# Token sums taken from rows, the next head's work at other places, and a direct attention projection, in a float32 encoder layer on one core

## The chip, the core and the metric

The program runs on one core of one Trainium2 chip. The time of a run is the device time of that core in microseconds (us). The kernel before took 1615.31 us, the median of three runs (1612.32 to 1615.61). The engines are named as the profile names them: PE (TensorE, matmul) with PEld (its weight loads), DVE (VectorE), ACT (ScalarE), POOL (GpSimd) and SP (SyncE, which issues nearly all transfers here).

## The reference

One encoder layer on x of 1024 tokens by 1024 features, all in float32. Two branches are computed from one projection, gated, added, and projected back.

```python
h = rms_norm(x, g_pre)
u_a, v_a, z_a, q_b, k_b, v_b, z_b, gate_a, gate_b = split(h @ w_in)    # 1024 -> 12288
y_a = spatial_gating(gelu(u_a), gelu(v_a), ln_g, ln_b, w_s, b_s) * silu(z_a)   # 2048 wide
y_b = mixture_of_dilations(q_b, k_b, v_b) * silu(z_b)    # 8 heads of 128, dilations 1, 4, 16
g_a, g_b = sigmoid(gate_a + b_gate[:1024]), sigmoid(gate_b + b_gate[1024:])
m = g_a * (y_a @ w_pa) + g_b * (y_b @ w_pb)
out = x + rms_norm(m @ w_o, g_post)
```

Each token attends, in each of three patterns, to 64 positions on both sides at a stride of 1, 4 or 16; the three results are combined by their softmax denominators.

## The kernel before

A float32 factor is kept as two parts, hi and lo: ACT copies the value to a rounded type (hi, L159, L106 for weights), and DVE or POOL subtracts it from the value (lo, L160, L108). A product is three matmuls: hi by hi, hi by lo, lo by hi. Nearly all of them multiply a 128x128 block by 128x512 into a PSUM bank of 128x512; there are eight banks.

The token matrix h is stored transposed, feature blocks on the partitions, in quarters hT[j][b]: j is the half of the features, b the half of the tokens. Most projections are not done directly, but by the seven products of Strassen's scheme on the 2x2 quarters, named p1, p6, p2, p7, p5, p4, p3 in that order; they need sums of token quarters (t1 to t4) and sums of weight quarters (s1 to s4, rows of the name ws_...).

The program has these stages, and pools of SBUF memory are opened and closed with them.

- Start (L202 to L330). norm_tile(c) takes one of eight chunks of 128 tokens, normalises it (ACT squares, DVE L230), transposes it on PE (L235) and splits it into hT. spatial_weights(q) prepares the spatial weights. Then v_b, which is needed in token rows, is computed directly by rows_product: chunk groups (0,1), (2,3), (4..7) with the first 512 columns, then (0..3) and (4..7) with the second. v_out splits the result into vh and vl (L160) and stores them; that frees the bank. Norms are emitted between the k steps of the first groups, and the four calls of sum_tile (L245) between those of the last two groups. sum_tile(k) adds hi and lo of a feature block on POOL (L251), forms t3, t2, t4, t1 on DVE (L257) and splits them.
- Projections (to 1033 us), seven products per block of 128 columns; gates(0) is the first. The change leaves this stage alone.
- Heads (to 1408 us). For each of eight heads weigh(h) runs nine stages: PE transposes the softmax weights (tiles st), they are split into pth and ptl (ptla for the chunked patterns), and multiplied with the values. Beside them run the next head's scores, a number of pairs of PSUM halves per stage (PAIRS), its exchange of maxima and sums between partitions, its normalise (which ends in scaling all its weights, L697 on DVE for eight of the tiles), and a number of steps of the other branch's product y_a @ w_pa (matmuls L844 to L846, bank pa, called steps).
- Tail. y_b times silu(z_b) is formed on POOL (L910) from o_d and z_d in DRAM, w_pb is read in quarters of 1 MB, and y_b @ w_pb runs as seven products (L1031 to L1033, pbp). gated() multiplies by the gate (thb), adds the other branch (mb, L987) and splits. Then the output product m @ w_o with wo's parts from DRAM (L1081 to L1083), the last norm and the residual, two chunks of tokens at a time.

The order on each engine comes from the scheduler of the language: it takes instructions of the program by their place in it, and may move one ahead where its inputs are ready in its model. Within an engine, instructions run in the order so fixed; an instruction that waits holds back all behind it, and so does a transfer in SP's queue. Tiles of a tag share a fixed number of buffers (bufs): a new one waits until the old content is no longer read.

Of the kernel before, what the change touches and what calls it, by code (L numbers as in the profile page):

```python
# [13 lines left out]
ALU = mybir.AluOpType  # L14
# [22 lines left out]
def tile_hybrid_encoder(  # L37
# [164 lines left out]
    with tc.tile_pool(name="start", bufs=1) as sp:  # L202
        xts, stored = [], []

        def load_tile(c):
            xt = sp.tile([P, D], F32, tag="xt", bufs=2, name=f"xt{c}")
            nc.sync.dma_start(xt, x_t[c])
            xts.append(xt)

        load_tile(0)  # L210
# [8 lines left out]
        def norm_tile(c, ahead=2):  # L219
            b, i = divmod(c, 4)  # L220
            for d in range(len(xts), min(c + ahead, 8)):
                load_tile(d)
            xt = xts[c]
            ss = sp.tile([P, 2], F32, tag="ss", bufs=2, name=f"ss{c}")
            xn = sp.tile([P, D], F32, tag="xn", bufs=2, name=f"xn{c}")
            nc.scalar.activation(xn, xt, AF.Square, accum_out=ss[:, 0:1])
            power(ss[:, 1:2], ss[:, 0:1], 1.0 / D)
            for j in range(2):
                gs = slice(512 * j, 512 * (j + 1))
                nc.vector.scalar_tensor_tensor(xn[:, gs], xt[:, gs], ss[:, 1:2], gpre[:, gs], op0=ALU.mult,  # L230
                                               op1=ALU.mult)
                pt = bank("pv", f"xT{c}{j}")
                for k in range(4):
                    kk = 4 * j + k
                    nc.tensor.transpose(pt[:, k * P:(k + 1) * P], xn[:, kk * P:(kk + 1) * P], ident)  # L235
                split(*[t[:, :, i * P:(i + 1) * P] for t in hT[j][b]], pt.rearrange("p (k n) -> p k n", k=4))

        def v_out(c, cb, ps):
            vh = sp.tile([P, 512], F32R, tag="vh", bufs=2, name=f"vh{cb}{c}")
# [5 lines left out]
        def sum_tile(k):  # L245

            xs = {}
            for j in range(2):
                for b in range(2):
                    xs[j, b] = sp.tile([P, 512], F32, tag=f"x{j}{b}", bufs=1, name=f"x{j}{b}_{k}")  # L250
                    nc.gpsimd.tensor_tensor(xs[j, b], f32(hT[j][b][0][:, k, :]), f32(hT[j][b][1][:, k, :]), ALU.add)  # L251
            t2 = sp.tile([P, 512], F32, tag="ssum", bufs=1, name=f"t2f{k}")
            for n, s, first, second, op in (("t3", xs[1, 1], xs[1, 1], xs[0, 1], ALU.subtract),
                                            ("t2", t2, xs[1, 1], xs[0, 0], ALU.add),
                                            ("t4", xs[1, 0], xs[1, 0], t2, ALU.subtract),
                                            ("t1", xs[0, 1], xs[0, 1], xs[0, 0], ALU.subtract)):
                nc.vector.tensor_tensor(s, first, second, op)  # L257
                if n in R:
                    split(R[n][0][:, k, :], R[n][1][:, k, :], s)
                else:  # L260
                    hl = [sp.tile([P, 512], F32R, tag=f"ss{q}", bufs=1, name=f"{n}{q}{k}") for q in "hl"]
                    split(*hl, s)
                    for t, d in zip(hl, t4_d):
                        nc.sync.dma_start(d[:, k, :], f32(t))
# [35 lines left out]
        for k in range(0, KT, 2):  # L300
            if k == 2:
                norm_tile(1, 1)
            wv += row_pair(w_in, OFF_VB, k, "vb0", (nc.gpsimd, nc.vector) if k < 4 else (nc.gpsimd, nc.gpsimd))
            if k == 0:
                load_tile(1)
            spatial_weights(k // 2)
        for cb, cs, tags in ((0, (0, 1), "mm mm"), (0, (2, 3), "sc sc"), (0, (4, 5, 6, 7), "sc tp mm mm"),
                             (1, (0, 1, 2, 3), "sc sc sc tp"), (1, (4, 5, 6, 7), "mm mm sc sc")):
            ahead = {}
            if cb == 0 and cs[0] < 4:  # L310
                ahead = {2: lambda: norm_tile(2), 5: lambda: norm_tile(3)} if cs[0] == 0 else \
                    {2 * i: (lambda c=4 + i: norm_tile(c)) for i in range(4)}
# [8 lines left out]
            if (cb, cs[0]) == (0, 4):  # L321
# [814 lines left out]
```

## Time and profile before

| What | us |
|---|---|
| median of three runs | 1615.31 |
| profiled execution | 1610.12 |
| its span, first to last instruction | 1608.3 |
| PE busy | 1508.8 |
| start, to the end of v_b | 0 to 147 |
| projections | 147 to 1033 |
| heads | 1033 to 1408.7 |
| attention projection, seven products | 1408.7 to 1499.3 |
| output product and end | 1499.3 to 1608.3 |

The profile is that of one execution. A row of the view in time order gives the start, the duration, the engine and line, the operation, "out<-in" by the program's names, the shape, and in brackets how long the engine was idle before it and what it waited for. A row of the grouped view has the busy time and the mean duration in ns of one, then the idle time before the group. A row of the transfers has the number, KB of each, and the median us from issue to landing. Matmuls overlap, so the distance of two starts counts and not the duration in the row. Lines are those of the kernel before.

### The profile page before, as it was taken

The numbers are of one execution on the slowest core, as the hardware profiler recorded it, in microseconds if no ns is written. First come the engines' busy times: TensorE is split into PE (matmuls) and PEld (weight loads), VectorE is DVE, ScalarE is ACT, GpSimd is POOL, SyncE is SP. The second block draws the span as 40 slices with busy tenths as digits, with TensorE's granted clock in tenths as the row PEclk, the third lists the DMA queues.
The fourth block names the chain that finished last, engine by engine and source line by source line (L and its number), as shares of the span: only waits on it lengthen the run. The fifth ranks groups of instructions, "written<-read, shape, count | busy, mean of one in ns | idle before, by whom it ended". The sixth has DMA issues, their size and how long they took to land.

```text
span 1608.3 us, 22594 instructions
## 1 busy us (share of the span) xinstructions
PE 1508.8 (94%) x7751; PEld 1264.2 (79%) x7751; DVE 934.6 (58%) x1698; ACT 716.0 (45%) x1391; POOL 818.5 (51%) x723
## 2 busy tenths in 40 slices
PE   8959999999999999999999999989998899789798
PEld 4747999988888888788788888767877777677586
DVE  5852544476675765757565655566666554596412
ACT  5422533343433434443354544677776665144111
POOL 3542644465555555565555555364344433687432
PEclk8979999999999999999999999999999999999899
DMA  8335433334534443536243343676666665924631
GB/s 263 136 125 191 150 106 105 111 125 133 162 125 144 135 147 116 180 102 193 99 159 130 121 148 110 217 227 196 194 198 179 207 188 168 334 97 144 235 105 66
DMA packets 238467, 252.14 MB, mean 157 GB/s; under 512 B 14056, under 2 KB 174856, under 8 KB 238096
## 3 DMA queue, kind: packets, MB, share of 16 engines
q1 hardware_dynamic: 238128, 250.14, 48.8%
q8 instruction: 61, 1.00, 0.3%
q10 hardware_dynamic: 224, 0.56, 0.1%
q14 instruction: 54, 0.44, 0.1%
HBM read 174.10 MB, written 76.55 MB: 156 GB/s over the span
## 4 chain that ended last, share of the span: by engine, by line
PE 63%; DVE 13%; DMA 6%; ACT 6%; issue 6%; POOL 5%; SPq 1%; DVEq 0%; POOLq 0%; ACTq 0%
PE sg L515 2%; PE pa L845 1%; PE pa L844 1%; PE pa L846 1%; DMA wr_pa<-in_w_proj_a_dram 1%; DMA vn<-v_d 1%; DVE vn L504 1%; PE vb L154 1%; PE vb L156 1%; PE vb L155 1%; PE sc L650 1%; ACT st L657 1%; DVE y L919 1%; ACT qrh L159 1%; PE pr L731 1%
## 5 line engine op out<-in xcount | busy, mean ns | idle before, releaser
L108 POOL TENSOR_TENSOR wl_pa<-wr_pa,wh_pa 128x512 fp32r<-128x512 f32 x56 | 73.4, 1318 | 86.7 <-ACT wh_pa L106 69.4
L504 DVE TENSOR_SCALAR vn<-vn,mean,rstd 128x128 f32<-128x128 f32 x128 | 55.3, 486 | 34.9 <-DMA vn<-v_d 34.5
L657 ACT ACTIVATE st<-st,own 128x256 f32<-128x256 f32 (+1 forms) x128 | 63.0, 493 | 24.0 <-DVE own L653 23.4
L106 ACT ACTIVATE wh_pa<-wr_pa 128x512 fp32r<-128x512 f32 x64 | 38.7, 624 | 46.1 <-DMA wr_pa<-in_w_proj_a_dram 37.2
L671 POOL COPY oth<-own 32x4 f32<-32x4 f32 x128 | 25.1, 196 | 54.1 <-ACT st L657 49.8
L653 DVE CUSTOM_DVE_ANT_0 st<-sc,tb 128x256 f32<-128x256 f32 x64 | 25.6, 422 | 37.8 <-PE sc L652 27.4
L160 POOL TENSOR_TENSOR vl<-vn,vh 128x512 fp32r<-128x512 f32 x32 | 41.3, 1292 | 0.8 <-ACT vh L159 0.8
L1085 ACT ACTIVATE sq<-o 128x512 f32<-128x512 f32 x16 | 9.6, 599 | 70.5 <-PE o L1083 70.5
L160 POOL TENSOR_TENSOR qcl<-q,qch 128x512 fp32r<-128x512 f32 x16 | 24.8, 1552 | 29.7 <-ACT qch L159 29.6
L1061 DVE TENSOR_TENSOR sso<-sso 128x1 f32<-128x1 f32 x8 | 1.3, 159 | 63.5 <-ACT sq L1085 63.5
L159 ACT ACTIVATE mhp<-mb 128x512 fp32r<-128x512 f32 x16 | 10.1, 632 | 54.9 <-POOL mb L987 54.9
L160 DVE TENSOR_TENSOR vl<-vb,vh 128x512 fp32r<-128x512 f32 x16 | 10.8, 688 | 38.2 <-ACT vh L159 33.9
L165 POOL TENSOR_TENSOR sso<-sso,mhalf 128x1 f32<-128x1 f32 x8 | 4.4, 552 | 54.9 <-DVE sso L164 54.9
L108 POOL TENSOR_TENSOR wl_wos<-wr_wos,wh_wos 128x512 fp32r<-128x512 f32 x16 | 20.7, 1293 | 22.8 <-ACT wh_wos L106 22.8
L154 PE MATMUL vb<-wh_vb,hT00h 128*128 128x512 f32 x32 | 14.2, 445 | 18.7 <-DVE vl L160 18.7
L1081 PE MATMUL o<-woh,mhp 128*128 128x512 f32 x64 | 26.3, 414 | 5.8 <-DMA woh<-wo_h 5.8
L987 POOL TENSOR_TENSOR mb<-thb,mb 128x512 f32<-128x512 f32 x16 | 21.4, 1337 | 19.8 <-DVE thb L986 15.5
L160 DVE TENSOR_TENSOR ptla<-pa,ptha 128x512 fp32r<-128x512 f32 (+1 forms) x32 | 19.8, 618 | 17.7 <-ACT ptha L159 17.6
L910 POOL TENSOR_TENSOR y<-y,zf 128x1024 f32<-128x1024 f32 x8 | 24.0, 3006 | 11.5 <-DMA zf<-z_d 8.7
L1082 PE MATMUL o<-wol,mhp 128*128 128x512 f32 x64 | 26.8, 422 | 3.1 <-DMA wol<-wo_l 3.1
L650 PE MATMUL sc<-krh,qch 128*128 128x256 f32 (+2 forms) x80 | 24.3, 306 | 5.7 <-DVE own L653 5.2
L653 DVE CUSTOM_DVE_ANT_0 st<-sc,ta 128x256 f32<-128x256 f32 x48 | 20.0, 420 | 15.2 <-PE sc L652 7.3
(2695 smaller groups left out, 6073.0 us busy)
## 6 DMA issues: line engine op xcount, KB each, us to landing
wr_pa<-in_w_proj_a_dram SPq DMA_DIRECT2D x32, 512.0 KB, 5.4
wr_g<-in_w_in_dram SPq DMA_DIRECT2D x16, 512.0 KB, 3.8
wr_va<-in_w_in_dram SPq DMA_DIRECT2D x16, 512.0 KB, 3.8
wr_u<-in_w_in_dram SPq DMA_DIRECT2D x16, 512.0 KB, 3.7
wr_z<-in_w_in_dram SPq DMA_DIRECT2D x16, 512.0 KB, 4.2
vn<-v_d SPq DMA_DIRECT2D x32, 256.0 KB, 3.1
y_d<-s SPq DMA_DIRECT2D x32, 256.0 KB, 2.5
wr_yf<-y_d SPq DMA_DIRECT2D x16, 512.0 KB, 5.1
```

The costliest lines, as they stand in the source:

```text
L106: nc.scalar.activation(hi, src, AF.Copy)
L108: low.tensor_tensor(lo, src, f32(hi), ALU.subtract)
L154: nc.tensor.matmul(ps, lhs[k][0], rh, start=(k == 0), stop=False)
L159: nc.scalar.activation(hi, src, AF.Copy)
L160: low.tensor_tensor(lo, src, f32(hi), ALU.subtract)
L504: nc.vector.tensor_scalar(vn[:, c, :], vn[:, c, :], mean[:, 4 * b + c, 0:1], rstd[:, 4 * b + c:4 * b + c + 1], op0=ALU.subtract, op1=ALU.mult)
L515: nc.tensor.matmul(pg[:, 256 * c:256 * (c + 1)], w[:, 2 * cp + c, :], wst, start=(w is vh and c == 0), stop=(w is vl and c == 1), skip_gro ...
L650: nc.tensor.matmul(dst, lhs[0], rhs[0], start=True, stop=False)
L653: nc.vector.tensor_tensor_reduce(st[:, t, :n], ps[:, t, :n], bias, -1.0, -NEG, ALU.add, ALU.min, own[:, half, idx, 0:1])
L657: nc.scalar.activation(st[:, t, :n], st[:, t, :n], AF.Exp, bias=own[:, half, idx, 0:1], scale=-1.0, accum_out=own[:, half, idx, 1:2])
L1081: nc.tensor.matmul(ps, mhi, wh, start=(k == 0), stop=False)
L1082: nc.tensor.matmul(ps, mhi, wl, start=False, stop=False)
```

## The change

Three parts of the program are rewritten.

**Start.** The chunks are normalised in the order 0, 4, 1, 5, 2, 6, 3, 7, and six of them stay in SBUF. sum_tile(i) forms t1 to t4 from the normalised rows of the chunks i and 4+i (two operations on DVE, two on POOL), transposes each on PE, and splits from PSUM. The groups of v_b follow the pairs. vh takes buffers of the tag "ws", which the weight sums of the projections use too.

**Heads.** PAIRS moves the scores one stage earlier, the exchange starts at stage 3 and its second half is all on DVE, and the scaling of a head's weights is split by tile.

**Tail.** y_b @ w_pb is computed directly, column block by column block; y is formed in pieces of two heads by half of the tokens, with two buffers for o and one for z; wo is loaded during the products; the output loop runs over four chunks for each half of the columns.

```diff
+        ORDER = [0, 4, 1, 5, 2, 6, 3, 7]
...
+        def transposed(hl, i, src, name):
+            pt = bank("pv", name)
+            for k in range(4):
+                nc.tensor.transpose(pt[:, k * P:(k + 1) * P], src[:, k * P:(k + 1) * P], ident)
+            split(*[t[:, :, i * P:(i + 1) * P] for t in hl], pt.rearrange("p (k n) -> p k n", k=4))
...
-            vh = sp.tile([P, 512], F32R, tag="vh", bufs=2, name=f"vh{cb}{c}")
+            vh = wpool.tile([P, 512], F32R, tag="ws", bufs=2, name=f"vh{cb}{c}")
...
-        def sum_tile(k):
-            xs = {}
-            for j in range(2):
-                for b in range(2):
-                    xs[j, b] = sp.tile([P, 512], F32, tag=f"x{j}{b}", bufs=1, name=f"x{j}{b}_{k}")
-                    nc.gpsimd.tensor_tensor(xs[j, b], f32(hT[j][b][0][:, k, :]), f32(hT[j][b][1][:, k, :]), ALU.add)
...
+        def sum_tile(i):
+            x = {(j, b): xts[4 * b + i][:, 512 * j:512 * (j + 1)] for j in range(2) for b in range(2)}
+            t1, t2, t3, t4 = [scratch(t, f"{n}f{i}") for n, t in (("t1", "th"), ("t2", "sa"), ("t3", "sb"), ("t4", "sc"))]
+            for n, t, first, second, op, eng in (("t3", t3, x[1, 1], x[0, 1], ALU.subtract, nc.vector),
+                                                 ("t1", t1, x[0, 1], x[0, 0], ALU.subtract, nc.gpsimd),
+                                                 ("t2", t2, t3, x[0, 0], ALU.add, nc.vector),
+                                                 ("t4", t4, x[1, 0], t2, ALU.subtract, nc.gpsimd)):
+                eng.tensor_tensor(t, first, second, op)
+                if n in R:
+                    transposed(R[n], i, t, f"{n}T{i}")
...
-        for cb, cs, tags in ((0, (0, 1), "mm mm"), (0, (2, 3), "sc sc"), (0, (4, 5, 6, 7), "sc tp mm mm"),
-                             (1, (0, 1, 2, 3), "sc sc sc tp"), (1, (4, 5, 6, 7), "mm mm sc sc")):
...
+        for cb, cs, tags, ahead in ((0, (0, 4), "mm mm", {2: norm(1), 5: norm(5)}),
+                                    (0, (1, 5), "sc sc", {0: norm(2), 2: sums(0), 3: norm(6), 5: sums(1), 6: norm(3), 7: norm(7, 0)}),
+                                    (0, (2, 6, 3, 7), "sc tp mm mm", {3: sums(2)}),
+                                    (1, (0, 4, 1, 5), "sc sc sc tp", {3: sums(3)}),
+                                    (1, (2, 6, 3, 7), "mm mm sc sc", {})):
...
-                    if half == 0:
-                        nc.gpsimd.tensor_copy(dst, src)
-                    elif i % 2:
-                        nc.scalar.activation(dst, src, AF.Copy)
-                    else:
-                        nc.vector.tensor_copy(dst, src)
+                    (nc.gpsimd, nc.vector)[half].tensor_copy(dst, src)
...
+        TILES = [[(1, r), (1, 4 + r)] for r in range(4)] + [[(0, 0), (0, 1), (0, 2)], [(0, 3), (0, 4)], [(0, 7)],
+                                                           [(0, 5), (0, 6)], []]
...
-        PAIRS = (1, 2, 2, 1, 2, 0, 0, 0, 0)
+        PAIRS = (2, 2, 2, 2, 0, 0, 0, 0, 0)
...
+        def gated_heads(h, b):
+            bs = slice(512 * b, 512 * (b + 1))
+            o, z = [tp.tile([P, 2, 512], F32, tag=t, bufs=n, name=f"{t}{h}{b}") for t, n in (("o", 2), ("z", 1))]
+            for t, src in ((o, o_d), (z, z_d)):
+                nc.sync.dma_start(t, src[h:h + 2, :, bs].rearrange("k p n -> p k n"))
+            for i in range(2):
+                y[h + i, b] = [tp.tile([P, 512], F32R, name=f"y{s}{h + i}{b}") for s in "hl"]
+                nc.gpsimd.tensor_tensor(o[:, i, :], o[:, i, :], z[:, i, :], ALU.mult)
+                split(*y[h + i, b], o[:, i, :])
                 yield
...
+        for m in range(KT):
+            if m + 1 < KT:
+                wb[m + 1] = cols_block(w_pb, (m + 1) * P, 0, f"pb{m + 1}")
+            if m == 4:
+                load_o(0, range(3))
+            elif m == 7:
+                load_o(0, range(3, KT))
+            for b in range(2):
...
+                for k, (lh, ll) in enumerate(wb[m]):
+                    rh, rl = y[k, b]
+                    nc.tensor.matmul(ps, lh, rh, start=(k == 0), stop=False)
+                    nc.tensor.matmul(ps, lh, rl, start=False, stop=False)
+                    nc.tensor.matmul(ps, ll, rh, start=False, stop=(k == KT - 1))
+                nc.vector.tensor_tensor(th, th, ps, ALU.mult)
+                nc.gpsimd.tensor_tensor(ma, th, ma, ALU.add)
+                split(*[t[:, m % 4, :] for t in m_[m // 4][b]], ma)
+        load_o(1, range(KT))
...
+        for b in range(2):
             for i in range(2):
-                for c in (2 * cc, 2 * cc + 1):
+                for c in range(4 * b, 4 * b + 4):
```

How the order moves is shown at three places. A name in these rows carries a running number; xT is the bank of a transposed half chunk, t1T to t4T that of a sum. First DVE, at the end of the third group of v_b's products and the last sum. Before:

```order
L257 TENSOR_TENSOR x_3_1039<-x_3_1039,t2f_1043 128x512
L160 TENSOR_TENSOR t1l<-x_3_1037,t1h 128x512
L160 TENSOR_TENSOR vl_717<-vb_0_616,vh_716 128x512
L160 TENSOR_TENSOR vl_723<-vb_1_617,vh_722 128x512
L324 TENSOR_SCALAR bg_half<-rowsT 128x16
L325 COPY lng<-rowsT 128x16
L160 TENSOR_TENSOR t4l_1052<-x_3_1039,t4h_1051 128x512
L356 TENSOR_TENSOR ws_g0s_1164<-wr_g_1140,wr_g_1142 128x512
L356 TENSOR_TENSOR ws_g0s_1166<-ws_g0s_1164,wr_g_1140 128x512
```

And in the change:

```order
L160 TENSOR_TENSOR t2l<-t2T_773,t2h 128x4x128
L160 TENSOR_TENSOR t4l_782<-t4T_783,t4h_781 128x512
L160 TENSOR_TENSOR vl_853<-vb_0_712,vh_852 128x512
L160 TENSOR_TENSOR vl_859<-vb_1_713,vh_858 128x512
L332 TENSOR_SCALAR bg_half<-rowsT 128x16
L333 COPY lng<-rowsT 128x16
L160 TENSOR_TENSOR vl_865<-vb_2_714,vh_864 128x512
L160 TENSOR_TENSOR vl_871<-vb_3_715,vh_870 128x512
L160 TENSOR_TENSOR t3l<-t3T_965,t3h 128x4x128
```

The subtractions of the third group now stand behind the third of the four sums, with the fourth behind them, and the first sums of weights (ws_g0s) are no longer here. They follow the last group's subtractions:

```order
L160 TENSOR_TENSOR vl_1185<-vb_0_1084,vh_1184 128x512
L160 TENSOR_TENSOR vl_1191<-vb_1_1085,vh_1190 128x512
L160 TENSOR_TENSOR vl_1197<-vb_2_1086,vh_1196 128x512
L160 TENSOR_TENSOR vl_1203<-vb_3_1087,vh_1202 128x512
L364 TENSOR_TENSOR ws_g0s_1240<-wr_g_1216,wr_g_1218 128x512
L364 TENSOR_TENSOR ws_g0s_1242<-ws_g0s_1240,wr_g_1216 128x512
```

Second DVE in the first head, where the next head's weights are scaled and the last chunk's low half (ptla of 128x256) is made. Before:

```order
L691 SCALAR_TENSOR_TENSOR nm_10394<-nm_10394,dd_10393 128x16
L697 TENSOR_SCALAR st_10064<-st_10064,nm_10394 128x256
L697 TENSOR_SCALAR st_10103<-st_10103,nm_10394 128x256
L697 TENSOR_SCALAR st_10064<-st_10064,nm_10394 128x256
L697 TENSOR_SCALAR st_10103<-st_10103,nm_10394 128x256
L697 TENSOR_SCALAR st_10091<-st_10091,nm_10394 128x256
L697 TENSOR_SCALAR st_10134<-st_10134,nm_10394 128x256
L697 TENSOR_SCALAR st_10091<-st_10091,nm_10394 128x256
L697 TENSOR_SCALAR st_10134<-st_10134,nm_10394 128x256
L160 TENSOR_TENSOR ptla_10425<-pa_10421,ptha_10424 128x256
```

And in the change:

```order
L696 SCALAR_TENSOR_TENSOR nm_10470<-nm_10470,dd_10469 128x16
L704 TENSOR_SCALAR st_10130<-st_10130,nm_10470 128x256
L160 TENSOR_TENSOR ptla_10485<-pa_10481,ptha_10484 128x256
L704 TENSOR_SCALAR st_10171<-st_10171,nm_10470 128x256
L704 TENSOR_SCALAR st_10130<-st_10130,nm_10470 128x256
L704 TENSOR_SCALAR st_10171<-st_10171,nm_10470 128x256
L803 TENSOR_TENSOR o_10116<-pc_10404,o_10116 128x512
```

The low half moves ahead of seven of the eight scalings. The same happens in the third head; in the others it stood apart from them before.

Third SP's queue at the end of the heads, in the change, where o and z are the pieces of y_b, and ma_d<-tha stores a finished block of the other branch:

```order
L922 DMA z_13709<-z_d 128x2x512
L864 DMA ma_d<-tha_13690 128x512
L922 DMA o_13759<-o_d 128x2x512
L851 DMA tha_13819<-th_d 128x512
L922 DMA z_13760<-z_d 128x2x512
L922 DMA o_13798<-o_d 128x2x512
```

Each z load waits there until the piece before it is multiplied. Before, the place had transfers of 1 MB:

```order
L906 DMA y_13632<-o_d 128x4x512
L909 DMA zf_13634<-z_d 128x2x512
L909 DMA zf_13637<-z_d 128x2x512
L914 DMA pb_13640<-in_w_proj_b_dram 128x4x512
L113 DMA wr_pa_13656<-in_w_proj_a_dram 128x8x128
```

More of the change, by code (lines that the diff above doesn't have):

```diff
@@ L266, in tile_hybrid_encoder @@
+                    transposed(hl, 0, t, f"{n}T{i}")
+                    for t_, d in zip(hl, t4_d):
+                        stored.append(nc.sync.dma_start(d[:, :, i * P:(i + 1) * P], f32(t_)))
         col = sp.tile([P, 1], F32, name="col")
@@ L777, in weigh @@
             begun = []
-            for stage in [residue(r) for r in range(4)] + [chunk(1), chunk(3), ends(), chunk(5), chunk(7)]:
+            for i, stage in enumerate([residue(r) for r in range(4)] + [chunk(1), chunk(3), ends(), chunk(5), chunk(7)]):
                 next(stage)
@@ L865, in tile_hybrid_encoder @@
             take(steps, 1)
-        exchange(0, heads[0], 0)
-        exchange(0, heads[0], 1)
+        take(exchange(0, heads[0], 0))
+        take(exchange(0, heads[0], 1))
         normalise(0, heads[0])
+        for tile_ in TILES[0] + TILES[1]:
+            scale(heads[0], *tile_)
         for _ in queries_keys(1, heads[1]):
@@ L879, in tile_hybrid_encoder @@
                     residue_values(h + 1, heads[h + 1])
-                if more and i == 4:
-                    exchange(h + 1, heads[h + 1], 0)
-                if more and i == 6:
-                    exchange(h + 1, heads[h + 1], 1)
+                if more and i == 3:
+                    take(exchange(h + 1, heads[h + 1], 0))
+                    late = exchange(h + 1, heads[h + 1], 1)
+                if more and i in (5, 6):
+                    take(late, 1)
                 if more and i == 7:
                     normalise(h + 1, heads[h + 1])
+                if more and i == 8:
+                    for tile_ in TILES[0] + TILES[1]:
+                        scale(heads[h + 1], *tile_)
                 if i > 4:
@@ L912, in load_w @@
-        def load_w(i, j):
-            wq[i, j] = whole(f"q{i}{j}", f"pb{i}{j}")
-            nc.sync.dma_start(wq[i, j], w_pb[512 * j:512 * (j + 1), 512 * i:512 * (i + 1)].rearrange(
-                "(k p) n -> p k n", p=P))
-        def by_k(dst, first, second, op, eng=nc.vector):
-            for k in range(4):
-                eng.tensor_tensor(dst[:, k, :], first[:, k, :], second[:, k, :], op)
-                yield
-        load_y(0, 0)
-        load_w(1, 0)
-        load_w(1, 1)
-        take(steps, 8)
@@ L943, in tile_hybrid_encoder @@
+        ready = (_ for h in range(0, H, 2) for b in range(2) for _ in gated_heads(h, b))
+        wb = {}
+        for i in range(16):
+            take(ready, 1)
+            take(steps, 4)
+            if i == 8:
+                take(steps, 8)
         take(steps)
-        u2, u3 = [hpool.tile([P, 4, 512], F32, tag=t, name=f"u{t}") for t in ("r01h", "r10h")]
-        for q_, tag in (((0, 0), "r10l"), ((1, 0), "r01l")):
-            ml[q_] = hpool.tile([P, 4, 512], F32R, tag=tag, name=f"ml{tag}")
+        m_ = [[quarter(j, b, "m") for b in range(2)] for j in range(2)]
@@ L1054, in tile_hybrid_encoder, with load_o @@
-        load_o(0, range(4, 8))
-        gp = whole("y11", "gp")[:, 0:2, :].rearrange("p k n -> p (k n)")
+        wo = {}
+        def load_o(i, ks):
+            for k in ks:
+                if i == 0 and k > 2:
+                    wo[i, k] = [wpool.tile([P, 512], F32R, tag=f"w{s}", bufs=WB, name=f"wo{s}{k}") for s in "hl"]
+                else:
+                    wo[i, k] = [tp.tile([P, 512], F32R, tag=f"y{s}{k}0" if i else f"wo{s}{k}", name=f"wo{s}{i}{k}")
+                                for s in "hl"]
+                for s in range(2):
+                    nc.sync.dma_start(f32(wo[i, k][s]), wo_d[s][i, k])
```

250 lines of the change are left out of this document (67 added, 183 removed).

## Prediction

> **What bounds the kernel now.** I read the first parts of the page first, to see which engine fills the span.
>
> ```profile
> span 1608.3 us, 22594 instructions
> PE 1508.8 (94%) x7751; PEld 1264.2 (79%) x7751; DVE 934.6 (58%) x1698; ACT 716.0 (45%) x1391; POOL 818.5 (51%) x723
> PE 63%; DVE 13%; DMA 6%; ACT 6%; issue 6%; POOL 5%; SPq 1%; DVEq 0%; POOLq 0%; ACTq 0%
> ```
>
> TensorE (PE) is busy for 1508.8 of 1608.3 us. An added matmul therefore costs its full interval, and a gain has to come out of the 99.5 us in which PE is idle, or out of intervals that are longer than they need be. The view of busy time by stretch, cut at the borders of the program's stages, says where that time lies.
>
> ```profile
> 10.30:82.60 72.30, 69.50 (x319) 50.60 (x319) 56.03 (x73) 34.65 (x64) 33.67 (x27) 0.94 0.58 188
> 82.60:101.20 18.60, 0.00 (x0) 0.00 (x0) 17.38 (x17) 8.03 (x14) 13.60 (x10) 0.63 0.33 113
> 147.00:1033.00 886.00, 878.71 (x4612) 756.47 (x4611) 529.80 (x861) 374.58 (x604) 486.72 (x365) 1.00 0.43 138
> 1033.00:1408.70 375.70, 335.41 (x1894) 280.11 (x1893) 223.89 (x615) 237.52 (x593) 175.82 (x238) 0.96 0.70 214
> 1408.70:1499.30 90.60, 81.70 (x338) 63.84 (x337) 72.92 (x71) 34.62 (x63) 67.97 (x45) 0.96 0.40 132
> 1499.30:1524.30 25.00, 16.18 (x49) 10.75 (x48) 8.34 (x12) 4.46 (x8) 10.06 (x8) 0.80 0.77 266
> 1524.30:1601.00 76.70, 76.36 (x337) 62.90 (x336) 12.48 (x28) 9.88 (x29) 21.68 (x21) 1.00 0.23 79
> ```
>
> A row gives the stretch, its length, the busy time of PE, weight loads, DVE, ACT and POOL, then the granted clock, the DMA share and GB/s. Four places matter. From 82.6 to 101.2 PE does nothing. From 147 to 1033 it is full, and the change does not touch that stage. In the heads (1033 to 1408.7) it is idle for 40.3 us. In 1499.3:1524.3, the first 25 us of the output projection, it issued 49 matmuls and the clock was 0.80.
>
> The price of a matmul is the distance between starts, not the printed duration. The rows below are the first and last of 33 in a row without a wait: (69.53 - 62.28) / 32 = 0.2266 us. The other two are a group of four 128x128 transposes and the matmul behind it: 0.35 us, and the next start comes 0.32 later instead of 0.23, so a group costs 0.44 us.
>
> ```profile
> 62.28 0.39 PE L154 MATMUL vb<-wh_vb,hT01h 128*128 128x512 f32 x1
> 69.53 0.39 PE L156 MATMUL vb<-wh_vb,hT01l 128*128 128x512 f32 x1
> 53.35 0.60 PE L235 MATMUL xT<-ident,xn 128*128 128x128 f32 x4
> 53.70 0.48 PE L154 MATMUL vb<-wh_vb,hT10h 128*128 128x512 f32 x1
> ```
>
> **Part A, the start.** The idle 18.6 us, by the rows of PE and DVE in time order:
>
> ```profile
> 101.24 0.80 PE L154 MATMUL vb<-wh_vb,hT00h 128*128 128x512 f32 x1 [18.66 <-DVE vl L160]
> 103.96 0.58 PE L154 MATMUL vb<-wh_vb,hT00h 128*128 128x512 f32 x1
> 59.15 1.28 DVE L160 TENSOR_TENSOR vl<-vb,vh 128x512 fp32r<-128x512 f32 x2
> 60.63 0.69 DVE L257 TENSOR_TENSOR x<-x,x 128x512 f32<-128x512 f32 x1 [0.21 <-POOL x L251]
> 66.57 1.78 DVE L160 TENSOR_TENSOR t1l<-x,t1h 128x512 fp32r<-128x512 f32 x1
> 100.50 1.27 DVE L160 TENSOR_TENSOR vl<-vb,vh 128x512 fp32r<-128x512 f32 x2
> 102.47 0.68 DVE L356 TENSOR_TENSOR ws_g0s<-wr_g,wr_g 128x512 f32<-128x512 f32 x1
> L230 DVE SCALAR_TENSOR_TENSOR xn<-xt,ss,gpre 128x512 f32<-128x512 f32 x16 | 13.6, 868 | 4.3 <-POOL ss L165 4.3
> ```
>
> The four sum_tile chains run on DVE and POOL from 60.63 to 102.5, one behind the other. The two vl subtractions that empty the PSUM banks for the next product stand behind them in DVE's queue (100.50), so PE waits 18.66 us, and its next six intervals take 103.96 - 101.24 = 2.72 us in place of 1.36 at a lower clock: 1.4 more. What goes: in the changed order the vl rows stand directly behind their product and the chains are spread over the stages before: **-18.7 -1.4 = -20.1**.
>
> What comes on PE: the four sums of four chunk pairs are transposed there, 16 groups of four, 16 x 0.44 = **+7.0**; nothing hides them.
>
> What comes on DVE: from the second product to the end of the third it has 46 operations of 128x512 where PE has 144 matmuls (32.6 us) and 22 groups of transposes (9.7): 42.3 us. Of the 46, 28 read PSUM and start about 0.6 us apart (59.15: two in 1.28); 18 read SBUF alone and take 0.6 to 1.7, as t1l's 1.78 beside x's 0.69 shows. So DVE needs 28 to 48 us, and up to 56 with a dozen hand-overs of 0.7 (the idle time before L230 is of that kind). PE, which now waits for these operands in its own queue, loses between 0 and 14 us. The mean of L230, 868 ns, lies in the lower third, but the hand-overs are serial: I take the middle, **+7**.
>
> A new wait: the high halves vh now live in the two "ws" buffers, which the first two weight sums of gates(0) also use. Before, these were made at 102.47, 44 us ahead of their use. Now they wait for the last vh to be stored, behind the last product. Without the wait the seven-product stage loses nothing; the chain store 2.1, two sums 1.4, high part 0.6, POOL low part 1.3 (the rows below) is 5.4 us, against 2.7 us of PE work in the first product p1: 2.7 us of stall, and 1.4 of low clock: **+4** (0 to 6). DVE's later sums and u2 evictions queue behind it, which is why I don't take less. Start together: -20.1 + 7.0 + 7 + 4 = **-2**, between -13 and +7.
>
> ```profile
> vb_h<-vh SPq DMA_DIRECT2D x16, 256.0 KB, 2.1
> L108 POOL TENSOR_TENSOR wl_pa<-wr_pa,wh_pa 128x512 fp32r<-128x512 f32 x56 | 73.4, 1318 | 86.7 <-ACT wh_pa L106 69.4
> L106 ACT ACTIVATE wh_pa<-wr_pa 128x512 fp32r<-128x512 f32 x64 | 38.7, 624 | 46.1 <-DMA wr_pa<-in_w_proj_a_dram 37.2
> ```
>
> **Part B, the heads.** The order of both kernels differs little on PE, so most of the 40 us of stalls stay. One place changes.
>
> ```profile
> 1102.54 2.84 DVE L697 TENSOR_SCALAR st<-st,nm 128x256 f32<-128x256 f32 x8
> 1105.31 0.41 DVE L160 TENSOR_TENSOR ptla<-pa,ptha 128x256 fp32r<-128x256 f32 x1
> 1105.77 0.39 PE L746 MATMUL pc<-ptla,va 128*128 128x256 f32 x1 [2.53 <-DVE ptla L160]
> 1177.31 0.39 PE L746 MATMUL pc<-ptla,va 128*128 128x256 f32 x1 [2.63 <-DVE ptla L160]
> ```
>
> In two heads the low half that PE waits for stood behind all eight scalings of the next head; in the new order behind one. 2.84 x 7/8 = 2.5 us earlier, of which the stall can give 2.2 to 2.5: 2 x 2.2 = -4.4. The scores come one step earlier (pairs 2,2,2,2), and half 1 of the exchange is all on DVE: eight copies more a head there, eight fewer on ACT, 0.2 us each (L671's POOL copies take 196 ns). I put that at nothing, since DVE is 60% busy in this stretch (223.89 of 375.70); if each copy lay on the path it would be 8 x 8 x 0.2 = 13 us, less the same on ACT. **-5**, between -10 and +4.
>
> ```profile
> L671 POOL COPY oth<-own 32x4 f32<-32x4 f32 x128 | 25.1, 196 | 54.1 <-ACT st L657 49.8
> ```
>
> **Part C, the tail.** The attention projection had seven products of 4x4x3 matmuls, 336; direct it has 8x2x8x3 = 384: 48 x 0.2266 = **+10.9**. From 1387 to 1600.5 the old tail took 213.5 us: the rest of pa, then 336 + 384 matmuls, 163.2 at full pace. The difference lies in rows like these.
>
> ```profile
> 1384.12 8.24 POOL L910 TENSOR_TENSOR y<-y,zf 128x1024 f32<-128x1024 f32 x2 [8.68 <-DMA zf<-z_d]
> 1393.63 0.79 PE L846 MATMUL pa<-ya1201h,wl_pa 128*128 128x512 f32 x1 [5.13 <-POOL wl_pa L108]
> 1397.64 0.57 PE L846 MATMUL pa<-ya1201h,wl_pa 128*128 128x512 f32 x1
> 1402.24 0.50 PE L844 MATMUL pa<-ya1201h,wh_pa 128*128 128x512 f32 x1 [1.30 <-ACT wh_pa L106]
> L1081 PE MATMUL o<-woh,mhp 128*128 128x512 f32 x64 | 26.3, 414 | 5.8 <-DMA woh<-wo_h 5.8
> L1082 PE MATMUL o<-wol,mhp 128*128 128x512 f32 x64 | 26.8, 422 | 3.1 <-DMA wol<-wo_l 3.1
> L987 POOL TENSOR_TENSOR mb<-thb,mb 128x512 f32<-128x512 f32 x16 | 21.4, 1337 | 19.8 <-DVE thb L986 15.5
> zf<-z_d SPq DMA_DIRECT2D x8, 512.0 KB, 12.3
> 1365.31 0.37 SPq L906 DMA_DIRECT2D y<-o_d  x1
> wr_g<-in_w_in_dram SPq DMA_DIRECT2D x16, 512.0 KB, 3.8
> ```
>
> (1) The output projection waited for wo. The new kernel loads wo[0] during the products, and wo[1] is needed only after four chunks, 96 x 0.2266 = 21.8 us later. The first 25.0 us held 49 matmuls, 11.1 at full pace: **-13.9**. What hides wo[1] are those 21.8 us; its 16 loads of 256 KB are 4.2 MB, 15.8 us at the stretch's 266 GB/s.
>
> (2) POOL's pair of y<-y,zf of 8.24 us stood ahead of wl_pa, whence the 5.13 us, nine intervals at low clock behind it (1397.64 - 1393.63 = 4.0 in place of 2.0), and the 1.30 of the next tile. The pieces are now 128x512 and 1.3 us each (L987, same shape and operands in SBUF). Without the three the last pa product ends near 1399.7 in place of 1408.1: **-8.4**.
>
> (3) But y is now a chain on one z buffer: each of eight steps loads a z of 512 KB and multiplies twice, 2 x 1.3 = 2.6 us, and only then can the next z be issued. The load lies between 3.8 (wr_g, where the queue is quiet) and 12.3 (zf itself, with 1 MB loads ahead of it). Since each step keeps only a z and an o in flight, I take 4: 6.6 us a step. The first o load was issued at 1365.31, when the last head's room came free. From 1366 the seventh step, which the first product needs, ends near 1366 + 7 x 6.6 = 1412. Some z loads also stand in SP's queue behind ma_d stores that wait for pa products; at this period they are not late. PE starts the direct products at 1399.7, does the 18 matmuls of the first six heads until 1403.8, and stalls to 1412: 8.2, with 1.4 for the clock, and 1.2 where the eighth step is late again: **+10.8** in place of the old projection's own losses, which were 90.6 - 76.1 = 14.5: waits for sums of tokens and weights, **-14.5**. I leave +1.7 for new waits on POOL's low halves and evictions.
>
> Tail: +10.9 - 13.9 - 8.4 + 10.8 - 14.5 + 1.7 = -13.4, and the last half of the output leaves on ACT's queue, -0.3: **-14**, between -22 (no stall at the direct products) and +19 (z loads of 8 us, below).
>
> The Trainium skill, "DMA: Bandwidth & Descriptors", section "Bandwidth", speaks against this part: batch DMAs to at least 1 MiB to get three quarters of peak, and the change cuts y and w_proj_b from 1 MB to 512 KB pieces. Here the pieces' rate (512 KB in 3.8 us, 138 GB/s) does lie below what the heads' stretch moved on the mean, 214 GB/s; by the rule the sum would be that of the second rival.
>
> **Sum.** -2 - 5 - 14 = -21 us, on the profiled execution of 1610.12 us (span 1608.3): 1589. The runs' median, 1615.31, lies 5.2 above that execution, so I predict **1594**.
>
> **Rivals.**
>
> The start gives nothing, or loses (0.14). The chains were DVE's and POOL's work, and DVE was 93% busy in the gap (17.38 of 18.60). If the 18 SBUF operations keep taking 1.7 us because POOL runs beside them, and the hand-overs are serial, the +7 is +14 and the start ends at +5; for it speaks that the norm rows too had waits on POOL; against it, that 28 of 46 operations now read PSUM. 1594 + 7, and with the ws wait at its 6: 1603.
>
> The z chain starves PE, which ends slower than before (0.12). If a z load takes 8 us under the tail's traffic, the middle between 3.8 and 12.3, a step takes 10.6 and the seventh ends at 1366 + 7 x 10.6 = 1440, 28 later; the eighth adds 4 more: 1626, 11 above the median now. It decides from 9.7 us a step on (a load of 7.1): 8 x 3.1 = 24.5 us uses up the gain of 21 and the 3.2 that can be told apart. For it: the 12.3 us of the same load; against it: a much shorter queue.
>
> All covers hold (0.12): no stall at the first direct product, DVE keeps pace in the start (-7): 1594 - 8 - 5 = 1581.
>
> The heads keep their stalls, since PE's order changes little there (part of the forecast's spread): 1599, and with the copies on the path 1603.
>
> The forecast has 0.62, its own range 1584 to 1605.
>
> **How the numbers follow.** The range takes in the start's rival and all covers, and the near side of the starved chain: **1577 to 1614**. 0.2% is 3.2 us, what a measurement of this kernel can tell from no change. Faster: nearly all of 0.62, most of 0.14, all of 0.12, a sixth of the starved chain: **0.85**. Same: **0.06**, slower: **0.09**, mostly the z chain.
>
> **What would show it.** Start: no PE gap above 5 us before the first product with column block 1; 16 groups of transposes more; the second and third product some 10 us longer; a stall of 2 to 4 us in gates(0) behind ws_g0s. Heads: the two waits on ptla below 0.5. Tail: no wait on woh or wol at the output's start; one stall of about 8 us on y[6] or y[7] at the beginning of the direct products; 768 matmuls in about 175 us after it. The prediction is wrong if PE waits again and again for y in the tail, if DVE stays full until the fourth product, or if the heads move by more than 10 us.

## The result and the profile after

The changed kernel takes 1596.47 us, the median of four runs (1594.95 to 1599.92), against 1614.28 for the kernel before in the same comparison: a ratio of 0.9895, 95% interval 0.9878 to 0.9913. The forecast was 1594, a gain of 21.3 on the median of three known then; the gain came to 17.8. The profiled execution has a span of 1595.0 in place of 1608.3. The page's first parts:

```profile
span 1595.0 us, 22762 instructions
PE 1519.5 (95%) x7863; PEld 1277.7 (80%) x7863; DVE 882.6 (55%) x1706; ACT 689.7 (43%) x1315; POOL 769.4 (48%) x703
```

PE is busy for 10.7 us more, as the 48 added matmuls and 16 groups of transposes ask for (18 us by the forecast's prices; slow intervals that went would be the rest, which wasn't added up: the mean granted clock of the span rose from 0.976 to 0.982), and idle for 75.5 in place of 99.5. The view by stretch, cut near the same events as the stages of before:

```profile
10.50:89.40 78.90, 73.37 (x361) 53.13 (x361) 50.56 (x86) 42.98 (x89) 31.94 (x28) 0.96 0.62 193
89.40:135.06 45.66, 45.66 (x211) 37.83 (x211) 8.27 (x15) 8.34 (x14) 2.59 (x2) 1.00 0.33 115
135.06:163.40 28.34, 22.12 (x85) 17.29 (x84) 15.02 (x17) 12.26 (x22) 17.17 (x12) 0.88 0.78 270
1030.00:1356.40 326.40, 294.62 (x1723) 248.72 (x1722) 229.23 (x652) 214.87 (x515) 148.12 (x223) 0.96 0.67 200
1356.40:1398.30 41.90, 38.91 (x171) 31.57 (x170) 11.62 (x11) 11.34 (x20) 27.65 (x21) 1.00 0.74 223
1398.30:1499.40 101.10, 89.45 (x383) 72.28 (x382) 30.70 (x40) 20.60 (x34) 44.38 (x34) 0.95 0.68 217
1499.40:1587.30 87.90, 87.90 (x386) 71.94 (x384) 13.85 (x30) 10.96 (x31) 22.93 (x22) 1.00 0.26 93
```

The rows of the kernel before with the same cuts, where they were not shown yet:

```profile
101.20:144.96 43.76, 43.72 (x186) 36.08 (x187) 7.98 (x14) 6.69 (x11) 4.66 (x4) 0.96 0.31 112
144.96:165.70 20.74, 19.38 (x85) 15.69 (x84) 10.66 (x14) 8.85 (x15) 8.50 (x7) 1.00 0.95 335
1033.50:1359.10 325.60, 293.70 (x1723) 247.18 (x1722) 200.16 (x587) 229.28 (x578) 145.25 (x222) 0.97 0.67 201
1359.10:1408.70 49.60, 41.21 (x169) 32.44 (x168) 23.23 (x28) 7.74 (x14) 30.42 (x16) 0.93 0.87 299
1499.30:1600.60 101.30, 92.48 (x385) 73.65 (x383) 20.82 (x40) 14.09 (x36) 31.73 (x29) 0.95 0.36 125
```

| stretch | before | after | difference | forecast |
|---|---|---|---|---|
| start, with gates(0) | 165.7 | 163.4 | -2.3 | -2 |
| projections | 867.8 | 866.6 | -1.2 | 0 |
| heads, to the last head's products | 325.6 | 326.4 | +0.8 | -5 |
| rest of y_a @ w_pa | 49.7 | 41.4 | -8.3 | -8.4 |
| y_b @ w_pb | 90.6 | 101.6 | +11.1 | +8.9 |
| output product | 101.3 | 87.8 | -13.4 | -13.9 |
| end | 7.7 | 7.7 | 0 | -0.3 |
| span | 1608.3 | 1595.0 | -13.3 | -21 |

In the tail the table goes by the starts of PE's rows, which lie some tenths off the cuts of the view: the first matmul of y_b @ w_pb stands at 1408.79 before and at 1397.84 after, the first of the output product at 1499.34 and at 1499.47.

The waits of PE, longest in total first, before the change and after it:

```profile
PE vb L154 <- DVE vl L160: 18.7, 1, 18.7
PE sc L650 <- DVE own L653: 9.2, 11, 2.6
PE pc L746 <- DVE ptla L160: 8.1, 5, 2.6
```

```profile
PE sc L658 <- DVE own L661: 11.8, 11, 2.6
PE pb L977 <- ACT yh L159: 10.2, 1, 10.2
PE g0p L408 <- ACT wh_g0p L106: 6.0, 1, 6.0
PE pc L757 <- DVE ptla L160: 4.3, 4, 2.9
```

A row names who waits, for whom, the total, how often, and the longest. The wait of 18.7 us is gone, and two new single waits stand there: for y at the first direct product, and for the first weight sum at gates(0). The rows in time order place them:

```profile
143.90 0.79 PE L408 MATMUL g0p<-t2h,wh_g0p 128*128 128x512 f32 x1 [5.97 <-ACT wh_g0p L106]
149.81 0.39 PE L408 MATMUL g0p<-hT10h,wh_g0p 128*128 128x512 f32 x1
1412.62 0.80 PE L977 MATMUL pb<-yh,wh_pb 128*128 128x512 f32 x1 [10.17 <-ACT yh L159]
```

Behind the first, the twelve matmuls of p6 take 149.81 - 143.90 = 5.9 us in place of 2.7, with one more wait of 0.25 among them. The second comes at 1412.62; the forecast had the z chain end at 1412.

### The profile page after: what moved, and what is told of

Its sections match the earlier page's. It is cut to its first block, busy times and chain, and to the rows that moved or that the text cites. A ratio compares the mean times of both kernels' runs of the same rounds, so it can differ in the third digit from the quotient of the medians.

```text
span 1595.0 us, 22762 instructions
## 1 busy us (share of the span) xinstructions
PE 1519.5 (95%) x7863; PEld 1277.7 (80%) x7863; DVE 882.6 (55%) x1706; ACT 689.7 (43%) x1315; POOL 769.4 (48%) x703
## 5 line engine op out<-in xcount | busy, mean ns | idle before, releaser
L977 PE MATMUL pb<-yh,wh_pb 128*128 128x512 f32 x128 | 50.6, 396 | 10.2 <-ACT yh L159 10.2
L978 PE MATMUL pb<-yl,wh_pb 128*128 128x512 f32 x128 | 50.8, 397 | 1.5 <-DVE yl L160 1.4
L678 DVE COPY oth<-own 32x4 f32<-32x4 f32 x128 | 47.3, 369 | 5.6 <-ACT st L665 3.5
L979 PE MATMUL pb<-yh,wl_pb 128*128 128x512 f32 x128 | 50.3, 393 | 0.0
L160 DVE TENSOR_TENSOR yl<-o,yh 128x512 fp32r<-128x512 f32 x16 | 18.2, 1135 | 39.4 <-ACT yh L159 38.7
L977 PEld LDWEIGHTS pb<-yh,wh_pb 128*128 128x128 f32 x128 | 24.4, 191 | 16.1 <-ACT yh L159 11.0
L658 PE MATMUL sc<-krh,qch 128*128 128x256 f32 (+1 forms) x80 | 24.6, 309 | 8.2 <-DVE own L661 7.6
```

The source lines that it names most:

```text
L160: low.tensor_tensor(lo, src, f32(hi), ALU.subtract)
L658: nc.tensor.matmul(dst, lhs[0], rhs[0], start=True, stop=False)
L678: (nc.gpsimd, nc.vector)[half].tensor_copy(dst, src)
L977: nc.tensor.matmul(ps, lh, rh, start=(k == 0), stop=False)
L978: nc.tensor.matmul(ps, lh, rl, start=False, stop=False)
L979: nc.tensor.matmul(ps, ll, rh, start=False, stop=(k == KT - 1))
```

## The experiments

All are the changed kernel with one edit, unless said otherwise. Times are medians; the ratio is to the kernel before.

**The wait at gates(0).** The two sums get other buffers than vh.

```diff
+            weights_of = weight_operands(..., name, (wpool, "th" if name == "g0" else "ws"))
```

> The changed kernel, except that the first two weight sums of gates(0) take the two free "th" buffers and no longer share "ws" with vh. Theory (the 5.97 us wait at gates(0) is the shared buffer, and about 1.5 us of low clock follow it): the wait falls below 1 us and the kernel gains 6 to 8 us on the changed one (1596.5), so about 1589. Rival (the wait is for weights that are loaded late, or for ACT and POOL behind the last group): the wait stays at 4 to 6 us, and the time within 2 us of 1596.

Measured: 1591.80 us, ratio 0.9868 (0.9846 to 0.9890), 4 to 5 us less than the change; the intervals of the two still overlap. In the profile the 5.97 us wait is gone, and one of 3.34 us stands at the product behind it, p2, with matmuls 0.43 us apart from there on:

```profile
142.87 0.65 PE L409 MATMUL g0p<-hT10h,wh_g0p 128*128 128x512 f32 x1 [3.34 <-ACT g0u L384]
145.45 0.63 PE L409 MATMUL g0p<-hT10h,wh_g0p 128*128 128x512 f32 x1
```

The shared buffer is shown to be the cause of the wait. The gain fell short of 6 because the next operation in line, ACT's eviction of p1's bank (g0u), which the kernel before also waited 1.36 us for, is now the late one: ACT's row has it waiting 3.29 us for a store of vl.

**The z chain.** Two z buffers; one pair of wo less has buffers of its own, to make room.

```diff
-            ... for t, n in (("o", 2), ("z", 1))]
+            ... for t, n in (("o", 2), ("z", 2))]
```

> The changed kernel with two z buffers in place of one; for the room, two and not three pairs of wo[0] have buffers of their own. Theory (the 10.2 us wait for y is the chain over one z buffer, 6.9 us a step): a step falls to 4 to 5 us, the wait below 3 us, and the kernel gains 7 to 10 us, about 1588. Rival (the transfers themselves, or POOL, which also makes the low parts of w_proj_b, set the pace): the wait stays above 6 us and the gain below 4.

Measured: 1594.91 us, 0.9885 (0.9864 to 0.9905): 1.6 less than the change. By the time alone the rival holds. The profile says otherwise. POOL's multiplications in the changed kernel, first and seventh of eight pairs, and the same two here:

```profile
1369.39 2.53 POOL L925 TENSOR_TENSOR o<-o,z 128x512 f32<-128x512 f32 x2 [3.01 <-DMA z<-z_d]
1410.65 2.49 POOL L925 TENSOR_TENSOR o<-o,z 128x512 f32<-128x512 f32 x2 [1.02 <-issue]
```

```profile
1368.68 2.54 POOL L925 TENSOR_TENSOR o<-o,z 128x512 f32<-128x512 f32 x2 [2.73 <-DMA z<-z_d]
1398.12 3.03 POOL L925 TENSOR_TENSOR o<-o,z 128x512 f32<-128x512 f32 x2 [0.70 <-DVE yl L160]
1399.24 0.46 SPq L113 DMA_DIRECT2D wr_pb<-in_w_proj_b_dram  x1
1408.19 0.79 PE L977 MATMUL pb<-yh,wh_pb 128*128 128x512 f32 x1 [12.89 <-ACT wh_pb L106]
```

A step fell from 41.26 / 6 = 6.9 us to 29.44 / 6 = 4.9. But the scheduler now put the whole chain ahead in SP's queue, and the first w_proj_b block was asked for at 1399.24 only: PE waits 12.89 us for its weights in place of 10.17 for y. So a further run adds to the two z buffers only this, that the first block's load is emitted earlier:

```diff
             take(ready, 1)
+            if i == 8:
+                wb[0] = cols_block(w_pb, 0, 0, "pb0")
             take(steps, 4)
```

> The changed kernel with two z buffers, as in the run with two z buffers before, and the first column block of w_proj_b asked for earlier in the program, so that its load stands in SP's queue between the y pieces and not behind all of them. Theory (two z buffers do speed the y chain; that run gained only 1.5 us since the wait went over to the first weights, 12.9 us for wh_pb): the wait at the first direct product falls below 5 us and the kernel is 5 to 9 us faster than the changed one, about 1589. Rival (the transfers set the pace, whichever comes first): a wait of 8 us or more stays, for y or for weights, and the gain is below 3.

Measured: 1585.05 us, 0.9826 (0.9806 to 0.9845), 11 less than the change and more than the 5 to 9 that were expected. The waits that are left there:

```profile
1400.57 0.49 PE L978 MATMUL pb<-yh,wh_pb 128*128 128x512 f32 x1 [0.68 <-ACT yh L159]
1402.13 0.71 PE L979 MATMUL pb<-yl,wh_pb 128*128 128x512 f32 x1 [1.07 <-DVE yl L160]
```

The single z buffer was the cause of the wait for y, and at that step the transfers were not the bound.

**The same wait, from PE's side.** The chain stays as it is; PE's queue is written in another order, so that three blocks' matmuls with the six heads that are ready come before any with the last two.

```diff
+        for m in range(3):
...
+            begun[m] = next_bank(f"pb0{m}")
+            multiply(begun[m], m, 0, range(6))
```

> The changed kernel; the first three column blocks' products for the first half of the tokens are begun with the six heads that are ready, and get the last two heads after that. The transfers and POOL's work keep their order. Theory (PE waits 10 us since its queue holds 54 matmuls that could run behind 6 that cannot; the chain of y itself need not get faster): the wait at the first product falls from 10.2 to 0 to 3 us, and the kernel gains 7 to 11 us on the changed one, about 1587. Rival (the direct products also starve on the y pieces of the second half of the tokens, or on POOL's low parts of the weights): the wait is split over later products and the gain is below 4.

Measured: 1587.79 us, 0.9847 (0.9816 to 0.9877), 8 to 9 less than the change. PE's longest wait for y is 2.4 us:

```profile
PE pb L969 <- ACT yh L159: 2.4, 1, 2.4
```

**The heads.** First the odd copies of the exchange go back to ACT:

```diff
-                    (nc.gpsimd, nc.vector)[half].tensor_copy(dst, src)
+                    if half and i % 2:
+                        nc.scalar.activation(dst, src, AF.Copy)
+                    else:
+                        (nc.gpsimd, nc.vector)[half].tensor_copy(dst, src)
```

> The changed kernel, with the copies of odd i in the second half of the exchange on ACT, as before the change; all else of the heads stays. Theory (the gain of the heads, 5 us from the two waits on ptla, went to 64 more copies on DVE, which take 0.37 us each where POOL runs beside them and stand ahead of the low halves): the heads get 3 to 6 us shorter, about 1592. Rival (the scores that come a stage earlier give the new waits on own and ptle): within 1.5 us of 1596.

Measured: 1591.14 us, 0.9862 (0.9840 to 0.9884), 5 less; the heads, from the first product of y_a to the last head's last (1030.1 to 1350.6), take 320.5 us against 326.1. The place where the changed kernel loses, DVE, POOL and PE in one head:

```profile
1283.87 3.69 DVE L678 COPY oth<-own 32x4 f32<-32x4 f32 x8
1287.58 0.42 DVE L160 TENSOR_TENSOR ptle<-pe,pthe 64x256 fp32r<-64x256 f32 x1
1284.59 1.53 POOL L160 TENSOR_TENSOR qcl<-q,qch 128x512 fp32r<-128x512 f32 x1 [3.48 <-ACT qch L159]
1286.06 1.29 POOL L108 TENSOR_TENSOR wl_pa<-wr_pa,wh_pa 128x512 fp32r<-128x512 f32 x1
1288.14 0.41 PE L723 MATMUL pa<-ident,st 128*128 128x128 f32 x2 [3.30 <-DVE ptle L160]
```

Eight copies of 32x4 elements take 3.69 us. The first five take 0.84 of it; the other three, beside POOL's two 128x512 subtractions, take 2.83. ptle, which PE waits 3.30 us for, stands behind them. With half of the copies on ACT:

```profile
1282.66 0.84 DVE L681 COPY oth<-own 32x4 f32<-32x4 f32 x5
1284.58 1.28 DVE L681 COPY oth<-own 32x4 f32<-32x4 f32 x2 [1.07 <-ACT st L665]
1285.89 0.42 DVE L160 TENSOR_TENSOR ptle<-pe,pthe 64x256 fp32r<-64x256 f32 x1
1286.45 0.41 PE L726 MATMUL pa<-ident,st 128*128 128x128 f32 x2 [1.15 <-DVE ptle L160]
```

The waits on own, which the rival names, stay: 13.9 us in all here, 11.8 in the change. In the four kernels with the old heads they are 8.5 to 9.6, so they come with the new order of the heads, whichever engine copies.

Then the heads of the kernel before, with the new start and tail (the diff is the whole part B, undone).

> The changed start and tail with the heads of the kernel before. Theory (the heads' part gives what it takes): the heads take 325 to 327 us as in both kernels, and the time is within 2 us of 1596, with the two waits of 2.5 us on ptla back. Rival (the heads' part is worth the 5 us forecast, and the profiled execution hides it): 1601.

Measured: 1599.04 us, 0.9914 (0.9889 to 0.9938), 3 more than the change, with overlapping intervals: between the two theories. The profiles say how to read it. The heads' length, cut as above, in the four kernels with the old heads was 325.3 (the kernel before), 328.6 here, and 328.3 and 329.6 in the two runs below; in the five with the new heads and DVE copies 326.1, 325.5, 323.1, 324.0 and 326.1. The means are 328.0 and 325.0. The heads in the profiled execution of before were the shortest of their kind, so the two profiles alone (+0.8) hide a gain of about 3 us, by one profile of each kernel. That accounts for most of the distance between the spans' 13.3 and the medians' 17.8; that it is all of it isn't shown.

**Start alone and tail alone**, each put into the kernel before.

> The kernel before with the start of the changed kernel alone. Theory (the 18.7 us wait is gone, but the transposes, DVE's pace and the wait at gates(0) take all but 2 to 3 us of it): 1 to 4 us faster than before, with the first va0 product 2 to 3 us earlier in the profile. Rival (the start gives its full 18.7 less 7 for the transposes, and another part loses it): 10 us faster.

Measured: 1607.58 us, 0.9974 (0.9958 to 0.9991): about 4 us faster, with the first va0 product at 162.8 in place of 165.7.

> The kernel before with the tail of the changed kernel alone. Theory (the tail carries nearly all of the gain): 9 to 14 us faster than before, with a wait for y of about 10 us at the first direct product, and none for wo in the output product. Rival (the tail's gain rests on the earlier end of the changed heads): less than 6 us faster.

Measured: 1601.62 us, 0.9930 (0.9911 to 0.9950): about 11 us faster, with the 10.2 us wait for y and none for wo. With 3 for the heads the parts add up to 18, the change as a whole gives 17 (0.9895).

**Three edits together**: the sums' buffers, the odd copies on ACT, the products begun early.

> Three edits on the changed kernel together: the weight sums of gates(0) in the th buffers, the odd copies on ACT, and the first three products begun early. Theory (three waits at three places, so the gains add: about 5 + 5 + 8): about 1578, ratio to before 0.977 to 0.981. Rival (an earlier end of the heads only lengthens the wait for y, since the chain starts when the last head's room comes free and heads and chain share POOL and the transfers): 1583 to 1588.

Measured: 1575.90 us, 0.9777 (0.9746 to 0.9808), 19 to 21 less than the change (by the ratios and by the medians) and the fastest of all. The gains add: the three alone come to 17 to 19. The heads take 318.8 us, and their earlier end moves the start of the y chain with it (the first o load goes out at 1350.80 in place of 1362.77), which is why the wait for y doesn't grow:

```profile
1399.95 0.50 PE L973 MATMUL pb<-yh,wh_pb 128*128 128x512 f32 x1 [1.68 <-ACT yh L159]
```

**All sixteen copies on ACT**, in that kernel.

> The kernel with the three edits together (1575.9 us), with all sixteen copies of the exchange's second half on ACT in place of eight. Theory (copies on DVE are slow beside POOL, 0.37 us on the mean and up to 1.6, on ACT they take 0.20 always): the heads lose another 1 to 4 us, about 1573. Rival (ACT's queue, with the high parts that PE waits for too, becomes the later one): the same or up to 3 us slower.

Measured: 1583.22 us, 0.9820 (0.9793 to 0.9847): 7 slower, the way of the rival and beyond its 3 us. On ACT each copy takes 0.20 us without exception, but the heads take 327.0 us in place of 318.8. Sixteen in one queue are 3.3 us, and ACT's own work stands behind them. PE's waits grow at several places, none of which is the whole: for the scaled weights (first row with eight copies on ACT, second with sixteen), for the next low half (third row, 0.8 with eight), and on own, 15.3 us in all for 13.4.

```profile
PE pb L727 <- DVE st L708: 4.3, 2, 4.1
PE pb L727 <- DVE st L708: 5.6, 2, 5.3
PE pb L727 <- DVE ptlb L160: 2.5, 1, 2.5
```

So waiting beside POOL is not the whole of the copies' price. Eight on each engine give heads of 318.8 us, sixteen on ACT 327.0, and sixteen on DVE gave 325.0 on the mean of the five kernels above. That the place in ACT's queue is the rest of the price is the likely reading; no run shows it by itself.

**Both cures of the y wait**, in the kernel with the three edits.

> The three edits together (1575.9 us), and with them two z buffers and the earlier first weights. Theory (both cures of the y wait act on the same 10 us, and the products begun early leave 1.7 and 0.6 us of it): the waits for y go to zero, gain 0 to 3 us, about 1574. Rival (the two cures act on different waits and add): 1567 or less. A third way: with the chain ahead, the second and third column blocks' weights come later than the products begun early want them, a new wait on wh_pb of 3 us or more, and 1578 or more.

Measured: 1584.16 us, 0.9809 (0.9775 to 0.9842), 5 to 8 slower (by the ratios and by the medians; the intervals overlap) than the three edits without them. It brought no gain that can be seen, and the profile shows the third way. Only the first block's weights were asked for early; the products begun early want the second and third too, and these now stand behind the y chain.

```profile
1401.49 0.79 PE L973 MATMUL pb<-yh,wh_pb 128*128 128x512 f32 x1 [9.64 <-ACT wh_pb L106]
```

## Why the prediction was right, and where its terms were not

**The size and the place of the gain** were right: the measured time lies 2.5 us above the forecast and inside the likeliest case's own range. The output product (-13.4 for -13.9), the rest of y_a @ w_pa (-8.3 for -8.4) and the wait for y (10.17 for 8.2) came as their steps had them, and the start came to -2.3 for -2. That the wait ended 0.6 us from the forecast instant is in part luck: the first o load went out at 1362.77 and not at 1366, but the first z took 6.2 us from issue to use and each later step 6.9 in all, where the working had 4 and 6.6.

Three figures of the working are off and change little. 8 x 3.1 is 24.8, not 24.5. All covers together, with -8 and -7, are 1579, not 1581. And the lower pace after the wait of 18.66 us held for seven intervals (101.24 to 104.38), 1.55 us more and not 1.4.

**The start was right by two errors that cancel.** DVE's pace was taken as +7, the middle of 0 to 14. The first matmul with column block 1 stands at 80.90 before, since six of them ran ahead of the long wait, and at 89.52 after:

```profile
80.90 0.50 PE L154 MATMUL vb<-wh_vb,hT00h 128*128 128x512 f32 x1
89.52 0.50 PE L154 MATMUL vb<-wh_vb,hT00h 128*128 128x512 f32 x1
```

So the three groups up to it took 79.0 us in place of 70.6, 8.4 more, of which twelve groups of transposes are 5.3: the pace cost some 3. What the prediction took as open, whether the 18 SBUF operations run at 0.7 or 1.7 us, the rows of the changed kernel settle: nearly all ran at the low end. The grouped view of DVE between 40 and 90 us has them as

```profile
L245 DVE SCALAR_TENSOR_TENSOR xt<-xt,ss,gpre 128x512 f32<-128x512 f32 x10 | 8.2, 847 | 3.2 <-POOL ss L165 3.2
L264 DVE TENSOR_TENSOR t2f<-t3f,xt 128x512 f32<-128x512 f32 x4 | 2.7, 679 | 0.3 <-issue 0.3
L264 DVE TENSOR_TENSOR t3f<-xt 128x512 f32<-128x512 f32 x3 | 2.1, 685 | 4.2 <-PE t3T L229 4.2
```

POOL's sixteen additions of hi and lo, beside which the old sums took 1.78, are gone with the old chains. The prediction had counted their removal only as an end of the chains, and not that the operations on DVE would be faster without them. The wait at gates(0) went the other way: +7.6 (28.34 against 20.74) for +4. The chain was put at 5.4 us from one store of vh. It starts later, since the last group's four vh, and its four vl, pass through two buffers each, so that the last ones themselves wait for stores; and the stores of vh took 3.9 us there as the median, where the sum had 2.1:

```profile
138.88 0.69 DVE L160 TENSOR_TENSOR vl<-vb,vh 128x512 fp32r<-128x512 f32 x1 [3.66 <-DMA vb_l<-vl]
139.33 0.60 ACT L159 ACTIVATE vh<-vb 128x512 fp32r<-128x512 f32 x1 [2.77 <-DMA vb_h<-vh]
142.44 0.69 DVE L364 TENSOR_TENSOR ws_g0s<-ws_g0s,wr_g 128x512 f32<-128x512 f32 x1 [1.19 <-DMA vb_h<-vh]
```

**The heads' step failed in its second half.** The two waits on ptla that it names are gone as forecast (the group's total went from 8.1 to 4.3 us; one of 2.86 now stands at 1294.66 in a later head, where six copies took 3.35 us on DVE just ahead). The step that put the eight more copies a head "at nothing, since DVE is 60% busy" is the one that was wrong: the share of busy time says nothing of what stands behind a copy, and the price of 0.2 us was POOL's. On DVE a copy took 0.37 on the mean:

```profile
L678 DVE COPY oth<-own 32x4 f32<-32x4 f32 x128 | 47.3, 369 | 5.6 <-ACT st L665 3.5
```

With half of them on ACT again, the heads gained the 5 us forecast and more (320.5, and 318.8 and 317.5 in two later runs, against a mean of 328.0).

**The direct products** came to +11.1 for +8.9, with the wait 2 us longer than forecast, mostly since PE reached it 1.4 us earlier. The step of the z chain took 6.9 us, not 6.6: 2.5 for the two multiplications, and 3.9 to 4.7 from a z's issue to its use, where the prediction had 4. One of the six:

```profile
1399.44 0.36 SPq L922 DMA_DIRECT2D z<-z_d  x1
1403.40 2.48 POOL L925 TENSOR_TENSOR o<-o,z 128x512 f32<-128x512 f32 x2 [0.60 <-DMA z<-z_d]
```

**The rival of the starved chain** didn't come: from a load of 7.1 us on it would have decided. The Trainium skill's rule on batches of at least 1 MiB ("DMA: Bandwidth & Descriptors", "Bandwidth") isn't settled by the rates here: the stretch moved 223 GB/s where that of before, with pieces of 1 MB and of 512 KB, moved 299, but SP's queue in the change also stood still for the one z buffer. The size of the pieces doesn't decide the time here: with the pieces unchanged and a second buffer, the chain's step fell by 2.0 us.

## What to carry to other kernels

Where a chain over one buffer is cured by a second one, look at what the scheduler then lets fall behind in the transfer queue: the wait here went from y to the weights, and the time alone hid that the step had become shorter. A cheap operation moved to an engine that isn't full must be priced by the rows of that engine beside its neighbours, and by what stands behind it in its queue. Matmuls that are ready behind matmuls that are not are a cheap cover for a late operand: changing their order gave 8 us and needed no new buffer, only three PSUM banks held open at once. And two cures of one wait need not add: here the time with both was 5 to 8 us longer than with the one.

## What the runs showed of the hardware

In the changed kernel a DVE copy of 32x4 elements takes 0.16 us as a rule (median 161 ns) and up to 1.56 beside POOL's subtractions; with all of them on ACT, the same copy took 188 to 209 ns in all 128 cases. The Trainium skill, "SBUF — State Buffer", section "Who interferes with whom", says that a DVE copy whose operands meet certain conditions can take the port pair it shares with GpSimd, and that one of the two then waits for the whole instruction of the other; the durations here, about as long as POOL's 1.29 to 1.53 us, agree. In the start, a DVE subtraction with two SBUF operands took 1.78 us beside POOL's additions and 0.68 without them.

The lower pace of matmuls after a wait, about 0.43 us from start to start where 0.227 is usual, goes with a granted clock of 0.50 to 0.51 in the two places looked at (143.9 to 149.8 in the change, 101.2 to 104.4 before it). It lasted for 12 intervals after the wait of 5.97 us, 10 after the one of 5.13 and 7 after the one of 18.66: its length doesn't follow the length of the wait. It still came after one of 3.34 us, and not after the one of 1.36 in the kernel before.
